# Eight rotations and 152 indexer heads read from matmul banks on VectorE, where a copy in SBUF was read

## The chip, the cores and the metric

One Trainium2 chip, one core. The metric is the device time of one execution in microseconds (us). The kernel before takes 3286.04 us, the median of 3 runs (3277.5 to 3291.01).

The engines are named as the profile names them: PE is the matmul engine (TensorE) and PEld its weight load, DVE is VectorE, ACT is ScalarE, POOL is GpSimd, SP is the engine that issues most of the transfers. PSUM is the memory that matmuls write, in banks of 128 partitions by 512 f32; SBUF is the working memory.

## What is computed

A decoder block over 2048 rows of 1024 channels. What matters here is the indexer of its sparse attention and the rotary embedding ahead of it:

```python
q  = partial_rope(q.reshape(bsz, seq, A_HEADS, HEAD_DIM), cos, sin)
k  = partial_rope(k[:, :, None, :], cos, sin)[:, :, 0]
qi = partial_rope(qi.reshape(bsz, seq, IDX_HEADS, IDX_DIM), cos, sin)
ki = partial_rope(ki[:, :, None, :], cos, sin)[:, :, 0]
...
# partial_rope: rot = [x1 * cos - x2 * sin, x2 * cos + x1 * sin] on 16 of 64 channels
rel   = jax.nn.relu(jnp.einsum('bqhd,bsd->bqhs', qib, ki))      # 4 indexer heads
score = jnp.einsum('bqh,bqhs->bqs', wib, rel)                   # weighted sum over heads
score = jnp.where(causal[None], score, -jnp.inf)
_, sel = lax.top_k(score, topk)                                 # 256 of up to 2048 keys
```

After this come attention over the selected keys, a convolution branch, an output projection, a cross-attention and a gated feed-forward part with a convolution.

## The kernel before, in words

Products are in three terms, of a high and a low part of each operand (`mm3`, lines 275 to 278). A weight tile is loaded, its high part is copied by ACT (L147) and its low part is the difference, on DVE (L152). PSUM has eight banks in four rings: `acc` (3 banks), `tr` (2, transposes), `s` (2) and `o` (1).

**Rotation** (`rotated`, L403 to L416, inside `proj_heads`). For each half of the rows and each of two groups of 512 rows, two pairs of products give the channels to be rotated: the first pair holds the indexer's and the key's channels (rows 0 to 47 of a bank are rotated), the other the queries' (rows 64 to 127). So there are 8 calls. A pair lies in two banks of `acc`, pa and pb. ACT copies both whole banks to SBUF (L406, L407). DVE makes four products with the cosine and sine tables (L410) from these copies, and writes the difference and the sum back over the rotated rows of the copies (L411, L412); what is not rotated is passed on by the copies. Then ACT and DVE split each copy into high and low parts (L147, L152, tile `both`), and SP stores them.

**Indexer scores** (`bg_scores`, L596 to L638). Keys go in stretches of 512; for each block of 128 queries that sees such a stretch there is a piece of four heads. A head is two matmuls into one bank (L615), of `s`, or of `o` for the third head of a piece where `deep` is set; a relu with the absolute weight as scale on ACT, from the bank to an SBUF tile r of a ring of three or four, or two (L617); and on DVE the first head's signed product (L619), or for the others a multiply-add into the sum sc (L621). Then ACT takes the sum apart into 16-bit keys (L633), DVE mends their sign (L634, L635), and SP stores them. `bg_select` loads the keys and searches the threshold by counting, on DVE (L687) or on ACT (L699).

There are 152 heads in three phases. **A**: query blocks 2 to 7, 10 pieces, 40 heads, deep, behind the projections at the start (105 to 215 us of the span). **B**: blocks 8 to 10, 9 pieces, 36 heads, not deep, tiles shared with the selection's (class `Places`, two tiles r), beside the attention of blocks 0 to 7 (up to about 785 us). **C**: blocks 11 to 15, 19 pieces, 76 heads, deep, four tiles r, beside a cross-attention (960 to 1075 us).

**Order of the work.** Each engine takes its queue in order. The program traces generators in turn (`interleave`, `Feed`), by estimated costs; the start, up to about 420 us, is a block whose queues are ordered at build time by a simulated timeline, with a priority for the scores (`later`, offset -SP). From 60 us on POOL works through a depthwise convolution (L958, L959), two instructions for each of 31 taps.

Of the kernel before, what the change touches and what calls it, by code (L numbers as in the profile page):

```python
# [8 lines left out]
F32 = mybir.dt.float32  # L9
# [12 lines left out]
P = 128  # L22
# [39 lines left out]
def hybrid_block(ctx: ExitStack, tc: tile.TileContext, x, mem, positions, norm_mix_g, w_in, w_heads, w_out,  # L62
# [30 lines left out]
    x, mem, out = x[0], mem[0], out[0]  # L93
# [33 lines left out]
    def load_r(dst, src):  # L127
        nc.sync.dma_start(out=dst.bitcast(F32), in_=src.bitcast(F32))
# [7 lines left out]
    def columns(src, h, t0, n):  # L136
        return src[t0 // 1024][:, h, t0 % 1024:t0 % 1024 + n]
# [7 lines left out]
    def split(hi, lo, src, eng=None):  # L145
        with held():
            i = S.activation(out=hi, in_=src, func=AF.Copy)  # L147
            if eng:
                eng.tensor_sub(out=lo, in0=src, in1=hi.bitcast(F32))
                note(S=i)  # L150
            else:
                note(S=i, V=V.tensor_sub(out=lo, in0=src, in1=hi.bitcast(F32)))  # L152
# [134 lines left out]
    def right(name, bufs=2):  # L287
        return tc.tile_pool(name=name, bufs=bufs, side="right", reuse_waits="tile")
# [94 lines left out]
    def proj_heads(ap, hs, half):  # L383
# [4 lines left out]
        RE = (G, V)[1]  # L388
        tabs = {}
# [3 lines left out]
        def send(dst, g, both, pieces):  # L393
            d = dst[half].rearrange("(a p) h t -> (p h) a t", a=2)[:, :, g * 512:(g + 1) * 512]
            for p0, r0, n in pieces:
                store_r(d[r0:r0 + n], both[p0:p0 + n])
# [6 lines left out]
        def rotated(dst, g, pa, pb, rows, pieces_a, pieces_b):  # L403
            ta, tb = (ap.tile([P, 512], F32, name=f"rot{i}", tag="rot", bufs=4) for i in "ab")
            tmps = [ap.tile([P, 512], F32, name=f"rp{i}", tag="rp", bufs=4) for i in range(4)]
            S.activation(out=ta, in_=pa, func=AF.Copy)  # L406
            S.activation(out=tb, in_=pb, func=AF.Copy)  # L407
            x1, x2, cos, sin = ta[rows], tb[rows], tabs[g][rows, 0], tabs[g][rows, 1]
            for o, i0, i1 in zip(tmps, (x1, x2, x2, x1), (cos, sin, cos, sin)):
                RE.tensor_mul(out=o[rows], in0=i0, in1=i1)  # L410
            RE.tensor_sub(out=x1, in0=tmps[0][rows], in1=tmps[1][rows])  # L411
            RE.tensor_add(out=x2, in0=tmps[2][rows], in1=tmps[3][rows])  # L412
            for t, pieces in ((ta, pieces_a), (tb, pieces_b)):
                both = ap.tile([P, 2, 512], F32R, name="both", tag="both", bufs=3)
                split(both[:, 0], both[:, 1], t)
                send(dst, g, both, pieces)  # L416
# [29 lines left out]
        def pair(dst, c0, rows, pieces_a, pieces_b):  # L446
            ws = [load_w(wh_v[:, :, c0 + i * P:c0 + (i + 1) * P]) for i in range(2)]
            for g in range(2):
                pss = []
                for w in ws:  # L450
                    pss.append(acc([P, 512]))
                    yield from product(pss[-1], w, g)
                    if waiting:
                        turn_values(*waiting.pop())
                    if rows is None:
                        plain(dst, g, pss[-1], (pieces_a, pieces_b)[len(pss) - 1])
                if rows is not None:
                    rotated(dst, g, *pss, rows, pieces_a, pieces_b)
# [101 lines left out]


    KP = 0
    SD = (True,4,2,2)

    class Parts:
# [30 lines left out]
    def bg_scores(ip, blks, deep=False, rb=3, sb=2, kb=2):  # L596

        for p0 in range(0, (blks[-1] + 1) * P, 512):
            pw = min(512, (blks[-1] + 1) * P - p0)
            ki2 = [ip.tile([P, 512], F32R, name="ki2", tag=f"ki2{a}", bufs=kb) for a in "ab"]  # L600
            for a in range(2):
                for h in range(2):
                    load_r(ki2[a][h * HD:(h + 1) * HD, :pw], columns(i_d, 4, p0, pw)[a * HD:(a + 1) * HD])
            for b in blks:
                n = (b + 1) * P
                w = min(512, n - p0)
                if w <= 0:
                    continue
                qi = ip.tile([P, NIH, P], F32R, name="qi", tag="qi")
                load_r(qi, columns(i_d, slice(0, NIH), b * P, P))  # L610
                sc = ip.tile([P, 512], F32, name="sc", tag="sc", bufs=sb)
                for h in range(NIH):
                    ps = (acc_o if deep and h % 3 == 2 else acc_s)([P, 512])
                    for a in range(2):
                        PE.matmul(ps[:, :w], qi[:, h, :], ki2[a][:, :w], start=a == 0, stop=a == 1)  # L615
                    r = ip.tile([P, 512], F32, name="r", tag="r", bufs=rb)
                    S.activation(out=r[:, :w], in_=ps[:, :w], func=AF.Relu, scale=absw[:, b, h:h + 1])  # L617
                    if h == 0:
                        V.tensor_scalar(out=sc[:, :w], in0=r[:, :w], scalar1=sgn[:, b, h:h + 1], scalar2=None, op0=ALU.mult)  # L619
                    else:  # L620
                        V.scalar_tensor_tensor(out=sc[:, :w], in0=r[:, :w], scalar=sgn[:, b, h:h + 1], in1=sc[:, :w],  # L621
                                               op0=ALU.mult, op1=ALU.add)
                if n - P >= p0 and n <= p0 + w:
                    V.tensor_add(out=sc[:, w - P:w], in0=sc[:, w - P:w], in1=cb2[:, P:])
                half = sc.bitcast(U16).rearrange("p (s e) -> p s e", e=2)
                hi = ip.tile([P, 512], U16, name="hi_w", tag="hi_w")
                lo = ip.tile([P, 512], U16, name="lo_w", tag="lo_w")
                m7 = ip.tile([P, 512], U16, name="m7", tag="m7", bufs=1)
                for c, a in ((hi, 1), (lo, 0)):
                    if deep and KP > a:  # L630
                        G.tensor_copy(out=c[:, :w], in_=half[:, :w, a])
                    else:
                        S.activation(out=c[:, :w], in_=half[:, :w, a], func=AF.Copy)  # L633
                V.tensor_scalar(out=m7[:, :w], in0=hi[:, :w], scalar1=32768.0, scalar2=32767.0, op0=ALU.is_ge, op1=ALU.mult)  # L634
                V.tensor_tensor(out=hi[:, :w], in0=hi[:, :w], in1=m7[:, :w], op=ALU.bitwise_xor)  # L635
                stq('Y').dma_start(out=key_d[0, b, :, p0:p0 + w], in_=hi[:, :w])
                stq('Y').dma_start(out=key_d[1, b, :, p0:p0 + w], in_=lo[:, :w])
                yield w * 5.5e-3  # L638
# [999 lines left out]
    def w_scores(blks):  # L1638
        return sum((b + 1) * P * 5.5e-3 for b in blks)
# [119 lines left out]
    with tc.block(schedule_with_timeline_sim=True), left("hd") as ap:  # L1759
# [88 lines left out]
        def behind():  # L1848
            with right("ti") as ip:
                yield from later(bg_scores(ip, list(range(2, 8)), True), -SP, False)  # L1850
            ts.append(Scope(right("ts")))
            yield from bg_select(ts[0].pool, *SEL0)
# [11 lines left out]
    with nullcontext() if SB == 8 else right("tx", bufs=1) as tx, right("kv") as kp:  # L1864

        def early_scores():
            drain(sel0)
            yield 0.0
            yield from later(bg_scores(Places(ts[0].pool, tx), list(range(8, SB))), 0, False)

        interleave(bg_attend(list(range(8)), load_kv(kp, 1024, early[1]), lambda b: False, early[2]), w_attend(range(8)), Feed(filler, W_GLU + 50 + 8 + 0 + (44 + -20 if OF0 else 0), 0),
                   Feed(sel0, 3 * w_select(*SEL0)), track.feed(1, 15),
                   *([Feed(early_scores(), 1 * w_scores(range(8, SB)), 40)] if SB > 8 else []))
# [8 lines left out]
    for half in range(2):  # L1882
# [34 lines left out]
        if half == 0:  # L1917
            last = cross(1, xb, hq)
            with right("ti") as ip:
                sc = Feed(bg_scores(ip, list(range(SB, 16)), *SD), 1.65 * w_scores(range(SB, 16)), 0)  # L1920
                done = 0.0
                while sc.live:
                    done += next(last)
                    sc.advance(done, W_CROSS)
# [86 lines left out]
```

## Time and profile before

| what | us |
|---|---|
| median of 3 runs | 3286.04 |
| the profiled execution, its own time | 3288.3 |
| its span in the trace | 3286.5 |
| PE busy | 3073.2 (94%) |
| DVE busy | 2464.3 (75%) |
| ACT busy | 1814.3 (55%) |
| POOL busy | 1339.2 (41%) |

Shares are of the span of one execution. A row of a group of instructions gives line, engine, operation, tiles, shape and count, then the busy time and the mean of one in ns, then the engine's idle time just before them and what ended it.

### The profile page before, as it was taken

Reading aid. Unit: us, or ns where it says so; the run is one execution under the profiler, and the core shown is the slowest. Engines: PE = TensorE matmul, PEld = TensorE weight load, DVE = VectorE, ACT = ScalarE, POOL = GpSimd, SP = SyncE. Lnnn points to the kernel's source line nnn. Section 1 sums busy time; section 2 is a strip of 40 time slices with the busy share of each in tenths; the row PEclk is TensorE's granted clock in tenths of the full one; section 3 lists DMA queues with packets and bytes.
Section 4 is the critical chain, followed back from the end, with each engine's and each line's share of the span. In section 5 each row is a group of like instructions: output and inputs, shape, how many; then the busy total and the mean of one; then the engine's idle time right before and its main releaser. Section 6 shows DMA issues by size and latency. Waiting matters only on the chain.

```text
span 3286.5 us, 45179 instructions
## 1 busy us (share of the span) xinstructions
PE 3073.2 (94%) x16162; PEld 2577.8 (78%) x16162; DVE 2464.3 (75%) x4852; ACT 1814.3 (55%) x3276; POOL 1339.2 (41%) x1141
## 2 busy tenths in 40 slices
PE   7987788998999998999999989999999999999998
PEld 5765577887877787788888878898878777777786
DVE  6899999877758678888788789986555766665445
ACT  7456467655458575667676668775443533333212
POOL 2999703999300799900000038992000144442000
PEclk9988899999999999999999999999999999999999
DMA  7452335543465312121221341103373322222432
GB/s 225 141 157 79 117 106 166 162 152 112 127 196 168 136 46 61 52 61 51 73 70 58 110 156 61 39 20 113 122 256 102 97 88 76 80 77 103 141 103 77
DMA packets 341960, 356.60 MB, mean 109 GB/s; under 512 B 21990, under 2 KB 268518, under 8 KB 340454
## 3 DMA queue, kind: packets, MB, share of 16 engines
q1 hardware_dynamic: 339302, 345.08, 33.2%
q0 software_dynamic: 2432, 8.64, 0.8%
q8 instruction: 127, 2.08, 0.3%
q14 instruction: 99, 0.81, 0.1%
HBM read 271.31 MB, written 82.34 MB: 108 GB/s over the span
## 4 chain that ended last, share of the span: by engine, by line
PE 53%; DVE 29%; ACT 9%; issue 5%; DMA 3%; SPq 0%; POOLq 0%; DVEq 0%; ACTq 0%
PE ps_w L1479 9%; PE ps_acc L276 6%; PE ps_acc L277 6%; PE ps_acc L278 6%; DVE jkc L687 5%; PE ps_s L277 4%; PE ps_s L278 4%; PE ps_s L276 4%; DVE wl L152 3%; ACT junk L699 3%; PE ps_acc L814 3%; DVE xa_cut L1511 2%; PE ps_tr L885 2%; DVE ca L1326 2%; PE ps_o L851 2%
## 5 line engine op out<-in xcount | busy, mean ns | idle before, releaser
L959 POOL TENSOR_TENSOR vt<-pr_c,vt 128x512 f32<-128x512 f32 x480 | 675.3, 1407 | 39.7
L152 DVE TENSOR_TENSOR wl<-raw,wh 128x1024 fp32r<-128x1024 f32 x252 | 335.2, 1331 | 223.1 <-ACT wh L147 217.9
L147 ACT ACTIVATE wh<-raw 128x1024 fp32r<-128x1024 f32 x252 | 264.7, 1051 | 376.5 <-PE ps_acc L278 176.4
L958 POOL TENSOR_SCALAR pr_c<-u,colsB 128x512 f32<-128x512 f32 x480 | 428.1, 892 | 45.1
L276 PE MATMUL ps_acc<-hp,wh 128*128 128x512 f32 x608 | 239.1, 395 | 1.2 <-ACT hp L322 0.8
L277 PE MATMUL ps_acc<-hp,wh 128*128 128x512 f32 x608 | 238.5, 392 | 0.8 <-DVE hp L323 0.8
L278 PE MATMUL ps_acc<-hp,wl 128*128 128x512 f32 x608 | 237.7, 392 | 0.0
L1252 POOL TENSOR_SCALAR xa<-xa,rs_y 128x1024 f32<-128x1024 f32 x4 | 4.4, 1124 | 504.5 <-DVE rs_y L170 504.5
L814 PE MATMUL ps_acc<-kst,qT 128*128 128x512 f32 (+3 forms) x624 | 180.5, 387 | 12.8 <-DVE mx L815 8.9
L836 ACT ACTIVATE prob<-prob,mx 128x1024 f32<-128x1024 f32 (+7 forms) x192 | 172.4, 899 | 27.5 <-DVE mx L815 27.1
L945 POOL DMA_DIRECT2D u<-u_d x16 | 9.3, 583 | 434.9 <-DMA key_d<-hi_w 223.3
L1454 POOL TENSOR_TENSOR hp_cut<-xb_cut 128x512 f32<-128x512 f32 x10 | 17.2, 1718 | 408.6 <-PE ps_tr L1400 352.1
L278 PE MATMUL ps_acc<-hh,wl 128*128 128x512 f32 (+1 forms) x384 | 158.5, 414 | 24.8 <-DVE wl L152 20.7
L317 ACT ACTIVATE pth<-ps_tr 128x512 fp32r<-128x512 f32 (+1 forms) x224 | 126.7, 574 | 91.2 <-PE ps_tr L885 81.7
L276 PE MATMUL ps_acc<-wh,hidh 128*128 128x256 f32 (+1 forms) x512 | 167.6, 327 | 7.1 <-ACT halo L1327 7.1
L1479 PE MATMUL ps_w<-T,wh 128*128 128x512 f32 x496 | 157.3, 399 | 17.9 <-DVE hp_cut L1490 17.9
L318 DVE TENSOR_TENSOR ptl<-ps_tr,pth 128x512 fp32r<-128x512 f32 (+1 forms) x224 | 145.8, 657 | 33.8 <-ACT pth L317 32.2
L276 PE MATMUL ps_acc<-hh,wh 128*128 128x512 f32 (+1 forms) x384 | 156.4, 413 | 15.2 <-ACT wh L147 12.3
L277 PE MATMUL ps_acc<-wl,hidh 128*128 128x256 f32 (+1 forms) x512 | 167.2, 327 | 0.0
L278 PE MATMUL ps_acc<-wh,hidl 128*128 128x256 f32 (+1 forms) x512 | 167.0, 326 | 0.0
L850 PE MATMUL ps_o<-pth,vst 128*128 128x256 f32 x544 | 159.8, 311 | 1.3 <-ACT y_c L991 1.0
L277 PE MATMUL ps_acc<-hl,wh 128*128 128x512 f32 (+1 forms) x384 | 158.8, 414 | 0.0
(479 smaller groups left out, 9891.8 us busy)
## 6 DMA issues: line engine op xcount, KB each, us to landing
raw<-in_w_down_dram SPq DMA_DIRECT2D x44, 512.0 KB
raw<-in_w_up_dram SPq DMA_DIRECT2D x34, 512.0 KB
raw<-in_w_gate_dram SPq DMA_DIRECT2D x34, 512.0 KB
raw<-in_w_out_dram SPq DMA_DIRECT2D x32, 512.0 KB
raw<-in_w_q_cross_dram SPq DMA_DIRECT2D x32, 512.0 KB
raw<-in_w_o_cross_dram SPq DMA_DIRECT2D x32, 512.0 KB
xt<-in_x_dram SPq DMA_DIRECT2D x24, 512.0 KB
raw<-in_w_in_dram SPq DMA_DIRECT2D x24, 512.0 KB
```

The costliest lines, as they stand in the source:

```text
L147: i = S.activation(out=hi, in_=src, func=AF.Copy)
L152: note(S=i, V=V.tensor_sub(out=lo, in0=src, in1=hi.bitcast(F32)))
L276: PE.matmul(ps, ah, bh, start=first, stop=False)
L277: PE.matmul(ps, ah, bl, start=False, stop=False)
L278: return PE.matmul(ps, al, bh, start=False, stop=last).ins
L687: V.tensor_scalar(out=tmp("jkc", n, U16), in0=key, scalar1=cand, scalar2=None, op0=ALU.is_ge, op1=ALU.add, accum_out=cnts[:, r:r + 1])
L814: PE.matmul(ps[:, :w], qT[:, hp * 2 + e, :], ks[p0 // 512][:, a, :w], start=a == 0, stop=a == 1)
L836: S.activation(out=pr, in_=pr, func=AF.Exp, scale=-1.0, bias=st["nm"][:, e:e + 1], accum_out=st["sm"][:, e, pi:pi + 1])
L850: PE.matmul(po, v, pth[:, j - j0, :], start=j == 0, stop=False)
L958: G.tensor_scalar(out=pr, in0=u[:, i:i + 512], scalar1=cb_w(i, c), scalar2=0.0, op0=ALU.mult, op1=ALU.add)
L959: G.tensor_add(out=vt[:, c, :], in0=pr, in1=vt[:, c, :])
L1479: PE.matmul(ps, x[:, k], y[:, k], start=first and k == i == 0, stop=k == 3 and i == 2, skip_group_check=True)
```

## The change

In the rotation, the four products read the rotated rows from the two matmul banks; the copies are still made, and the difference and the sum are written over their rotated rows. In the scores, the relu writes its result over the bank that it reads, and DVE reads the bank; the tile r is no longer allocated.

```diff
             S.activation(out=ta, in_=pa, func=AF.Copy)
             S.activation(out=tb, in_=pb, func=AF.Copy)
-            x1, x2, cos, sin = ta[rows], tb[rows], tabs[g][rows, 0], tabs[g][rows, 1]
+            x1, x2, cos, sin = pa[rows], pb[rows], tabs[g][rows, 0], tabs[g][rows, 1]
             for o, i0, i1 in zip(tmps, (x1, x2, x2, x1), (cos, sin, cos, sin)):
                 RE.tensor_mul(out=o[rows], in0=i0, in1=i1)
-            RE.tensor_sub(out=x1, in0=tmps[0][rows], in1=tmps[1][rows])
-            RE.tensor_add(out=x2, in0=tmps[2][rows], in1=tmps[3][rows])
+            RE.tensor_sub(out=ta[rows], in0=tmps[0][rows], in1=tmps[1][rows])
+            RE.tensor_add(out=tb[rows], in0=tmps[2][rows], in1=tmps[3][rows])
...
+    PR = 1
...
                     ps = (acc_o if deep and h % 3 == 2 else acc_s)([P, 512])
...
-                    r = ip.tile([P, 512], F32, name="r", tag="r", bufs=rb)
+                    r = ps if PR else ip.tile([P, 512], F32, name="r", tag="r", bufs=rb)
                     S.activation(out=r[:, :w], in_=ps[:, :w], func=AF.Relu, scale=absw[:, b, h:h + 1])
```

## Rows read from the trace of the kernel before

**Rows 1.** Busy us of each engine by stretch, then granted clock, DMA share, GB/s

```profile
110.00:160.00 50.00, 48.64 (x215) 39.25 (x213) 46.94 (x47) 25.74 (x43) 46.23 (x37) 1.00 0.46 136
160.00:215.00 55.00, 48.07 (x196) 38.77 (x195) 51.60 (x56) 24.48 (x47) 51.55 (x39) 0.88 0.53 151
215.00:300.00 85.00, 61.29 (x259) 47.32 (x258) 83.00 (x266) 48.98 (x100) 79.04 (x73) 0.86 0.37 105
300.00:420.00 120.00, 97.17 (x407) 73.94 (x406) 117.16 (x246) 71.07 (x154) 87.97 (x68) 0.91 0.38 115
...
740.00:790.00 50.00, 39.07 (x224) 30.33 (x223) 44.05 (x71) 31.77 (x61) 46.46 (x41) 0.97 0.30 90
...
960.00:1075.00 115.00, 111.66 (x543) 90.28 (x542) 93.11 (x189) 90.61 (x176) 0.00 (x0) 1.00 0.52 156
```

**Rows 2.** Waits by who waited for whom, 110 to 420 us: total, times, longest

```profile
PEld ps_acc L278 <- DVE wl L152: 29.6, 12, 6.1
...
PEld ps_tr L379 <- DVE hl L323: 13.7, 4, 10.9
...
PE ps_s L615 <- ACT r L617: 7.5, 4, 2.9
```

**Rows 3.** Groups by line on DVE, 105 to 215 us (phase A)

```profile
L621 DVE SCALAR_TENSOR_TENSOR sc<-r,sgn,sc 128x512 f32<-128x512 f32 (+3 forms) x30 | 34.1, 1137 | 2.0
...
L619 DVE TENSOR_SCALAR sc<-r,sgn 128x512 f32<-128x512 f32 (+3 forms) x10 | 8.8, 879 | 0.7 <-ACT r L617 0.7
```

**Rows 4.** Groups by line and shape on DVE, 960 to 1075 us (phase C)

```profile
L621 DVE SCALAR_TENSOR_TENSOR sc<-r,sgn,sc 128x512 f32<-128x512 f32 x48 | 35.7, 750 | 1.7 <-ACT r L617 0.2
L619 DVE TENSOR_SCALAR sc<-r,sgn 128x512 f32<-128x512 f32 x16 | 7.7, 482 | 0.7 <-ACT r L617 0.7
```

**Rows 5.** Lines 323 and 318, whole span: ns min/median/max, first and last start

```profile
L323 DVE SCALAR_TENSOR_TENSOR hl<-ps_tr,colsA,hh x32: 732/744/753, 17.9 to 311.3; 128x512 fp32r<-128x512 f32 x32
L323 DVE SCALAR_TENSOR_TENSOR ml<-ps_tr,colsA,mh x8: 469/479/484, 575.7 to 582.9; 128x256 fp32r<-128x256 f32 x8
...
L318 DVE TENSOR_TENSOR ptl<-ps_tr,pth x224: 410/684/703, 442.7 to 2538.4; 128x512 fp32r<-128x512 f32 x106, 128x256 fp32r<-128x256 f32 x6
```

**Rows 6.** Groups by line on DVE, 60 to 420 us: the rotation's products

```profile
L410 DVE TENSOR_TENSOR rp<-rotb,tab 48x512 f32<-48x512 f32 (+1 forms) x16 | 18.2, 1177 | 0.1
L410 DVE TENSOR_TENSOR rp<-rota,tab 48x512 f32<-48x512 f32 (+1 forms) x16 | 15.1, 944 | 4.4 <-ACT tab L263 4.3
```

**Rows 7.** Timeline of one head of phase A: start us, us, engine

```profile
152.01 0.62 PE L615 MATMUL ps_o<-ki,qi 128*128 128x512 f32 x2
...
164.40 0.68 ACT L617 ACTIVATE r<-ps_o,absw 128x512 f32<-128x512 f32 x1
...
169.94 2.75 DVE L621 SCALAR_TENSOR_TENSOR sc<-r,sgn,sc 128x512 f32<-128x512 f32 x2
```

**Rows 8.** Timeline of a rotation, 352 to 376 us: first bank copied, last product

```profile
352.44 0.59 ACT L406 ACTIVATE rota<-ps_acc 128x512 f32<-128x512 f32 x1
...
374.61 1.10 DVE L410 TENSOR_TENSOR rp<-rota,tab 64x512 f32<-64x512 f32 x1
```

**Rows 9.** Timeline of one head of phase B

```profile
754.13 0.63 PE L615 MATMUL ps_s<-ki,qi 128*128 128x512 f32 x2
...
756.94 0.85 DVE L619 TENSOR_SCALAR sc<-r,sgn 128x512 f32<-128x512 f32 x1
```

**Rows 10.** Timeline of phase C's first head

```profile
964.85 1.07 PE L615 MATMUL ps_s<-ki,qi 128*128 128x512 f32 x4
...
967.66 0.48 DVE L619 TENSOR_SCALAR sc<-r,sgn 128x512 f32<-128x512 f32 x1
```

**Rows 11.** Groups by line and shape on ACT, whole span: evacuations of a bank

```profile
L317 ACT ACTIVATE pth<-ps_tr 128x512 fp32r<-128x512 f32 x200 | 117.6, 598 | 89.8 <-PE ps_tr L885 80.2 <-PE ps_tr L1183 5.8 <-DVE o L874 1.7
L617 ACT ACTIVATE r<-ps_s,absw 128x512 f32<-128x512 f32 x90 | 59.9, 693 | 13.0 <-PE ps_s L615 6.7 <-DVE rs_y L170 4.1 <-DVE sc L621 1.2
...
L1323 ACT ACTIVATE ca<-ps_acc,colsA 128x512 f32<-128x512 f32 x22 | 16.7, 761 | 0.0
```

## The prediction

> **What bounds the kernel now.** I read the busy time by stretch first, because the change touches three short phases of a long kernel and an average over the span says nothing of them. From 110 to 420 us DVE is busy 298.7 of 310 us (46.94, 51.60, 83.00 and 117.16 added up), 96%, while PE, which is near full elsewhere, falls to 61 of 85 us and 97 of 120 us [rows 1]. There DVE sets the pace. The waits agree: PE's products stand for the low parts of weights (L152) and of the normed input (L323), both made on DVE [rows 2]. In phase C it is the other way round: PE is busy 111.66 of 115 us and DVE 93.11 [rows 1]. Phase B, at 740 to 790 us, is between: DVE 44, PE 39 of 50 us.
>
> Next, what the touched instructions cost in these phases. The multiply-add of a head (L621) takes a mean of 1137 ns in phase A and 750 ns at 512 columns in phase C; the first head's product (L619) 879 and 482 [rows 3, 4]. POOL is busy 46 of 50 and 52 of 55 us in phase A and not at all in phase C [rows 1]. So POOL's convolution, beside it, is what stretches DVE instructions whose tensors both lie in SBUF. Third, the same form with its first tensor in a bank: L323 runs from 18 to 311 us, most of it beside POOL, and takes 732 to 753 ns, with no long one among 32; the plain subtraction L318 takes 684 ns and at most 703 [rows 5]. A bank as first input escapes the stretching. That is the ground of the forecast.
>
> **Part 1, the scores on DVE.** Phase A has 30 multiply-adds and 10 first products. By the code six pieces meet the first 512 keys (one of 384 columns, five of 512) and four the next (128, 256, 384, 512): 6 of 10 are 512 wide, 2 are 384, one 256, one 128. From a bank a multiply-add costs 744 ns at 512 and 479 at 256 [rows 5], so 1.04 ns a column, hence 0.61 us at 384 and 0.35 at 128. Thirty: 18 x 0.744 + 6 x 0.61 + 3 x 0.479 + 3 x 0.35 = 19.5 us, against 34.1 [rows 3]: 14.6 less. The trace shows no first product (L619) that reads a bank. Its bounds are 482 ns, its price now without POOL [rows 4], and 744, the same width with one more tensor [rows 5]. I take 744, since reading 512 columns out of a bank costs 684 even in the plain subtraction: ten cost 6.5 us against 8.8 [rows 3], 2.3 less. Together 16.9 us of DVE time in phase A; with the lower price 19.
>
> In phase C nothing is gained: 750 becomes 744, and 19 first products cost up to 0.26 us more each, 5 us, which lie beside a PE that has the longer work; without that cover they would cost 5. Phase B's gain on DVE, at phase A's rate over 36 heads, would be about 15 us, but it is spread over stretches where PE has other work; I take 2.
>
> **Part 2, the rotation.** The 32 products take 18.2 + 15.1 = 33.3 us [rows 6]. From a bank each costs the plain subtraction's 0.684 [rows 5]: 21.9. Gain 11.4; the first eight, at about 72 to 85 us, lie ahead of the stretch that DVE sets, and a quarter of the count with the least stretching is some 1.5 us of it. So 9.9 count. The difference and the sum still have both inputs in SBUF and stay as they are.
>
> [...] The rows: 744 ns from a bank, 750 from SBUF, the same form and width [rows 4, 5]. [...]
>
> **Part 3, the relu that writes its bank.** No ACT row writes a bank. Bounds: 598 ns, the plain evacuation, and 761, the dearest evacuation to SBUF; now it is 693 [rows 11]. Times 152 heads that is 14 us less or 10 more on ACT, which is busy at most 91 of 115 us in the three phases [rows 1]: hidden. I take no change.
>
> **Part 4, the banks held longer.** This is the price. Now a bank is free once the relu has read it, and the ring of tiles r lets DVE lag; afterwards it is free when DVE has read it. Behind the matmuls of the next head (L615) PE has all its products queued. In phase A the head shown begins on PE at 152.01, ends on ACT at 165.08 and on DVE not before 171 [rows 7]: the hold grows by half. The wait for banks there is 7.5 us on PE already [rows 2]. Lower bound of the addition: none, since the build places matmuls by when their banks come free and DVE is quicker; upper bound: the wait three times over, 15 more, where the hold grows by half. I take 4, half of the present wait. In phase B two banks serve; the hold is 754.13 to 757.79, 3.7 us [rows 9], so a head is possible every 1.85 us. The 36 heads are spread over more than 100 us, and on average that fits; in bursts, a head's matmuls every 0.63 us, each could wait 1.2 us: bounds 0 and 44. I take 3, near the lower end, as part of the hold is a lag that shrinks when PE waits. In phase C the hold is 964.85 to 968.14, 3.3 us [rows 10]. Three of four heads go through two banks, so a bank takes 3 heads of 8 and a head is possible every 3 x 3.3 / 8 = 1.24 us. 76 heads in 115 us need one every 1.5: on average it fits, and the lower bound is none. In bursts, two matmuls every 0.6 us, each head could wait 0.64 us: upper bound 49. I take 4, near the lower end, because cross-attention products stand between the heads and can fill the wait.
>
> For the rotation a bank of three is held until the last product: at 352 to 376 us, 23 us in place of 0.6 [rows 8]. The next pair begins in the third bank, and its second product follows some 6 us later; bounds 0 and 2 us for each of 8. I take none, for DVE and not PE is late there, and it is what would show first if the cover were gone.
>
> **Sum.** In the stretch that DVE sets: 16.9 + 9.9 - 4 = 22.8 us, of which its 96% share, 22, is carried to the end. After it PE has the longer work, so time won stays won. B: 2 - 3 = -1. C: -4. Net 17 us less than the profiled execution's 3288.3, which is 2.3 above the median of the runs: 3288.3 - 17 - 2.3 = **3269 us**, 0.5% less. About 0.5% is also what a measurement of this kernel can tell from no change, so this forecast lies on the line; its own range is 3254 to 3282.
>
> **The rivals.**
>
> *PE waits for banks (slower).* Place: L615 in phase C, where PE is the bound. Price: at the upper bound of phase C 49 us in place of 4, and 8 in place of 3 in B: 50 more than forecast, 3319. It decides from a mean wait of 0.2 us for each of the 112 heads of B and C, which eats the 22 us of phase A. For it: nothing but three banks, and bursts. Against it: matmuls of other parts stand between the heads, and heads already wait behind the relu without much loss. Chance 0.18; half strength gives 3294.
>
> *DVE's gain goes nowhere.* The time is set in phase A by the chain from head to keys to search, not by DVE's sum; DVE idles more. Then only the waits are left of the terms: 3286, or up to 8 more. For it: PE is busy 48.64 of 50 us at 110 to 160 [rows 1], so there both are full. Against it: DVE is 96% busy for 300 us. Chance 0.20.
>
> *The change doesn't do what it says.* The multiply-add has a second tensor and a column in SBUF and stays stretched beside POOL. L323 has both too and isn't stretched. Then 14.6 us fall away: 3283, or 3275 if only half the stretching stays. Chance 0.05.
>
> *More than reckoned.* POOL, disturbed less, ends its taps sooner, fewer other DVE instructions are stretched, and the granted clock of 0.86 to 0.91 [rows 1] comes back as PE idles less: another 15 us, 3254. Chance 0.12.
>
> **How the numbers follow.** The forecast has 0.45. Of it a little over half lies below 3269.6, about 0.26; with the last case and a little of the fourth that is faster 0.40. Slower is most of the first rival, 0.15; the rest, 0.45, is within 0.5%. The range leaves out the bank rival's far end and a tenth on the low side: 3248 to 3302.
>
> **What would show it.** Right: L621 in phase A near 650 ns and never 1700, L410 near 684, DVE's 96% stretch shorter by some 20 us, so that the attention starts earlier; in phase C PE's waits for DVE at L615 of a few us in all. Wrong: L615 waiting for L621 by tens of us, or the stretch from 110 to 420 us as long as before with DVE idle in it.

## The result, and the profile after

| what | before | after |
|---|---|---|
| median of 5 runs, us | 3286.04 | 3267.32 (3263.5 to 3270.41) |
| profiled execution, its own time | 3288.3 | 3263.5 |
| its span | 3286.5 | 3261.7 |
| PE, DVE, ACT, POOL busy | 3073.2, 2464.3, 1814.3, 1339.2 | 3067.2, 2425.8, 1816.6, 1313.1 |

The ratio of the times is 0.9938, with an interval of 0.9927 to 0.9949: 0.6% faster, as forecast and 2 us below the forecast time. From L560 on, a line of the kernel after has a number one higher: the relu is L618, the first product L620, the multiply-add L622, the heads' matmuls L616.

The first check is on single instructions: is an operation that reads a bank free of the stretching beside POOL? These are the groups by line on DVE in the kernel after, from 105 to 215 us, against [rows 3]:

```profile
L622 DVE SCALAR_TENSOR_TENSOR sc<-ps_s,sgn,sc 128x512 f32<-128x512 f32 (+3 forms) x20 | 13.1, 653 | 3.9 <-ACT ps_s L618 3.2
L622 DVE SCALAR_TENSOR_TENSOR sc<-ps_o,sgn,sc 128x512 f32<-128x512 f32 (+3 forms) x10 | 6.6, 657 | 0.4
L620 DVE TENSOR_SCALAR sc<-ps_s,sgn 128x512 f32<-128x512 f32 (+3 forms) x10 | 6.5, 648 | 0.7 <-ACT ps_s L618 0.6
```

and these the instructions of three lines over the whole span (count, then ns min/median/max, first and last start):

```profile
L622 DVE SCALAR_TENSOR_TENSOR sc<-ps_s,sgn,sc x85: 338/742/753, 111.5 to 1057.8; 128x512 f32<-128x512 f32 x62, 128x384 f32<-128x384 f32 x9, 128x128 f32<-128x128 f32 x7, 128x256 f32<-128x256 f32 x7
L620 DVE TENSOR_SCALAR sc<-ps_s,sgn x38: 337/741/752, 110.7 to 1053.7; 128x512 f32<-128x512 f32 x28, 128x384 f32<-128x384 f32 x4, 128x128 f32<-128x128 f32 x3, 128x256 f32<-128x256 f32 x3
L410 DVE TENSOR_TENSOR rp<-ps_acc,tab x32: 670/684/697, 72.5 to 375.6; 48x512 f32<-48x512 f32 x16, 64x512 f32<-64x512 f32 x16
```

The thirty multiply-adds of phase A take 19.7 us in place of 34.1, the ten first products 6.5 in place of 8.8, and the longest of each line is within 2% of its median, though POOL is 46 of 50 us busy beside them. The rotation's products take 684 ns each and keep DVE busy for 20.6 us in all [rows 6: 33.3].

The second check is where the time went. Busy time by stretch in the kernel after (columns as in rows 1):

```profile
110.00:160.00 50.00, 50.00 (x225) 41.16 (x224) 40.15 (x53) 29.93 (x48) 46.21 (x42) 1.00 0.56 162
160.00:215.00 55.00, 54.84 (x257) 45.36 (x256) 47.09 (x76) 27.80 (x51) 51.09 (x44) 1.00 0.63 186
215.00:300.00 85.00, 57.25 (x242) 43.51 (x240) 84.79 (x267) 53.11 (x112) 78.97 (x75) 0.86 0.27 78
300.00:420.00 120.00, 101.36 (x404) 79.09 (x405) 109.95 (x246) 68.06 (x146) 68.77 (x54) 0.89 0.36 108
```

From 110 to 215 us the bound has changed hands. Before, PE was busy 96.7 of 105 us there [rows 1]; now it is busy 104.8, at full clock (1.00 in place of 0.88 in the second half), and DVE has 17.8 us to spare. The attention begins (first exponential) at 428.5 us; in the kernel before it began at 441.0. From 60 us to that point, before and then after:

```profile
60.00:441.00 381.00, 323.55 (x1380) 252.96 (x1380) 344.35 (x716) 200.18 (x395) 308.08 (x252) 0.92 0.43 125
```

```profile
60.00:428.50 368.50, 319.64 (x1384) 252.29 (x1382) 313.52 (x717) 203.15 (x396) 287.26 (x252) 0.93 0.45 130
```

DVE has 30.8 us less to do, the stretch is 12.5 us shorter, and the other 18.3 us have become DVE's idle time (36.7 before, 55.0 after); 11.3 of them lie between 110 and 215 us.

For the later stages I read marks in the two traces: the first exponential of the attention, the first maximum of the cross-attention (end of phase B), and the first multiply-add into the feed-forward part's channels, `ca`, from a bank of `acc` (L1326 before; phase C lies ahead of it).

| stage, us | before | after | difference | forecast |
|---|---|---|---|---|
| start to attention (rotation, phase A) | 441.0 | 428.5 | -12.5 | -22 |
| attention to cross-attention (B) | 363.7 | 357.4 | -6.3 | +1 |
| cross-attention to feed-forward (C) | 339.6 | 338.3 | -1.3 | +4 |
| the rest | 2142.2 | 2137.5 | -4.7 | 0 |

The first three add up to -20.1 where -17 was forecast: the total came out near, and its parts did not. The last row is no finding. Over the single profiles of before, after and the ten kernels below that keep the convolution, the same stretch takes from 2137.5 to 2147.5 us with no order that I can see.

### The profile page after: what moved, and what is told of

Read it like the earlier page. It is cut to its first block, busy times and chain, and to the rows that moved or that the text cites. A ratio compares the mean times of both kernels' runs of the same rounds, so it can differ in the third digit from the quotient of the medians.

```text
span 3261.7 us, 45167 instructions
## 1 busy us (share of the span) xinstructions
PE 3067.2 (94%) x16162; PEld 2578.6 (79%) x16162; DVE 2425.8 (74%) x4852; ACT 1816.6 (56%) x3276; POOL 1313.1 (40%) x1141
## 4 chain that ended last, share of the span: by engine, by line
PE 56%; DVE 27%; ACT 10%; issue 5%; DMA 2%; SPq 0%; POOLq 0%; DVEq 0%; ACTq 0%
PE ps_w L1480 9%; PE ps_acc L276 6%; PE ps_acc L278 6%; PE ps_acc L277 6%; DVE jkc L688 4%; PE ps_s L277 4%; PE ps_s L278 4%; PE ps_s L276 4%; DVE wl L152 3%; ACT junk L700 3%; PE ps_acc L815 3%; DVE xa_cut L1512 2%; PE ps_tr L886 2%; DVE ca L1327 2%; PE ps_o L852 2%
## 5 line engine op out<-in xcount | busy, mean ns | idle before, releaser
L960 POOL TENSOR_TENSOR vt<-pr_c,vt 128x512 f32<-128x512 f32 x480 | 665.3, 1386 | 39.6
L152 DVE TENSOR_TENSOR wl<-raw,wh 128x1024 fp32r<-128x1024 f32 x252 | 339.7, 1349 | 238.2 <-ACT wh L147 235.3
L959 POOL TENSOR_SCALAR pr_c<-u,colsB 128x512 f32<-128x512 f32 x480 | 413.1, 861 | 45.1
L276 PE MATMUL ps_acc<-hh,wh 128*128 128x512 f32 (+1 forms) x384 | 156.9, 414 | 17.1 <-DVE rp L410 10.4
L318 DVE TENSOR_TENSOR ptl<-ps_tr,pth 128x512 fp32r<-128x512 f32 (+1 forms) x224 | 145.6, 655 | 34.7 <-ACT pth L317 33.8
```

What stands on the lines that cost most here:

```text
L276: PE.matmul(ps, ah, bh, start=first, stop=False)
L318: note(S=ins, V=V.tensor_sub(out=lo, in0=ps, in1=hi.bitcast(F32)))
L959: G.tensor_scalar(out=pr, in0=u[:, i:i + 512], scalar1=cb_w(i, c), scalar2=0.0, op0=ALU.mult, op1=ALU.add)
L960: G.tensor_add(out=vt[:, c, :], in0=pr, in1=vt[:, c, :])
```

## The experiments

The theory: what is gained is relief of DVE from POOL, and what is paid is banks held longer. The rivals: that one part carries the whole gain and the other nothing, and that the gain has another source than POOL (another order of the queues, for one). Each kernel was timed in five rounds against the kernel before, which took 3289.58 us in the first batch (rotation alone, scores alone, A alone, rotation with A and B), 3289.77 in the second (B alone, the two without the convolution, the one without copies) and 3293.6 in the third, on another chip (the others). Across batches I compare ratios.

### The rotation alone, the scores alone

The first keeps the rotation's part of the change and gives the relu its tile r back:

```diff
-    PR = 1
+    PR = 0
```

> Only the rotation reads the banks; the scores keep their tile r. Stretching theory: the 32 products fall from 33.3 to about 22 us, of which some 9 reach the end: 3277, and L619/L621 stay stretched in phase A (near 1100 ns). Reordering theory (the gain comes from another order of the queues, not from shorter instructions): no relation to the 11 us, between 3265 and 3290. Banks theory (acc banks held too long): 3286 or more, with PE waiting for L410.

The second keeps the scores' part and lets the rotation read its copies again:

```diff
-            x1, x2, cos, sin = pa[rows], pb[rows], tabs[g][rows, 0], tabs[g][rows, 1]
+            x1, x2, cos, sin = ta[rows], tb[rows], tabs[g][rows, 0], tabs[g][rows, 1]
```

> All 152 heads use the bank, the rotation reads its copies as before. Less a_only this gives B and C together. Stretching theory: B has POOL beside it and gains some us, C has none and loses at most a few: 3270 to 3276. Banks theory: B and C lose, so this is slower than a_only by 5 us or more.

The rotation alone: 3295.55 us, ratio 1.0012 [1.0003, 1.0022], 0.1% slower. The scores alone: 3271.88 us, 0.994 [0.9927, 0.9954], as good as the whole change within the intervals.

The rotation alone gained nothing where 3277 us was expected; the heads stay stretched, 1212 ns for a multiply-add of phase A. DVE did get faster at its products: L410 takes 20.6 us there too. But PE waits for it. PE's and PEld's waits for it from 60 to 435 us (in us, how often, the longest), first in the kernel with the rotation alone:

```profile
PE ps_acc L276 <- DVE rp L410: 19.2, 5, 8.5
PEld ps_acc L276 <- DVE rp L410: 10.7, 2, 8.8
```

and in the kernel after:

```profile
PE ps_acc L276 <- DVE rp L410: 10.4, 2, 6.3
```

PEld's waits are the same pauses, seen at the weight load (from 200 to 300 us it is one of 8.8 us on PEld and one of 8.5 on PE), so the two are not added up: PE waits 19.2 us and 10.4 us.

One such wait in the rotation-only kernel, from its timelines of ACT, DVE and PE (start, us, engine; in brackets the idle time and what ended it):

```profile
359.18 0.60 ACT L406 ACTIVATE rota<-ps_acc 128x512 f32<-128x512 f32 x1 [3.49 <-PE ps_acc L278]
371.12 0.57 ACT L407 ACTIVATE rotb<-ps_acc 128x512 f32<-128x512 f32 x1
...
361.06 0.69 DVE L410 TENSOR_TENSOR rp<-ps_acc,tab 64x512 f32<-64x512 f32 x1
374.10 1.91 DVE L410 TENSOR_TENSOR rp<-ps_acc,tab 64x512 f32<-64x512 f32 x3
...
369.95 0.39 PE L278 MATMUL ps_acc<-hh,wl 128*128 128x512 f32 x1
375.54 0.77 PE L276 MATMUL ps_acc<-hh,wh 128*128 128x512 f32 x1 [5.20 <-DVE rp L410]
376.11 0.63 PE L277 MATMUL ps_acc<-hl,wh 128*128 128x512 f32 x1
```

The first bank is copied by 359.8 us, the second by 371.7; before the change each would, by the program, have been free then. Here PE's next product wants a bank at 370.3 and gets it at 375.5, when DVE has come round to its products, 13 us after the first of them. The matmuls that follow the pause take 0.63 us in place of 0.39. This is the row of the `acc` banks that the forecast priced at nothing.

### Phase A alone, B alone, both, and the rotation with both

```diff
-                    r = ps if PR else ip.tile([P, 512], F32, name="r", tag="r", bufs=rb)
+                    r = ps if blks[0] in (2,) else ip.tile([P, 512], F32, name="r", tag="r", bufs=rb)
```

The tuple is (2,) for phase A, (8,) for B, (2, 8) for both; a phase is known by its first query block. The first three also have the rotation reading its copies; the fourth has (2, 8) and the change's rotation.

> Only the 40 heads of phase A (blocks 2 to 7) use the bank; rotation, B and C as before. Stretching theory: L619 and L621 in phase A fall from 42.9 to about 26 us, the attention starts 10 to 14 us earlier, 3273. Banks theory: PE waits for DVE at L615 take back half or more: 3280 or above. Reordering theory: no relation.

> Only the 36 heads of phase B (blocks 8 to 10, beside the attention of blocks 0 to 7) use the bank; rotation, A and C as before. scores_only less a_only left 13 us to B and C, where B was reckoned at 1. Theory that B carries them: 3274 to 3280, and the stage from the first exponential to the first maximum of the cross-attention is 5 to 8 us shorter than the 364 us of the kernel before. Theory that parts do not add up and B is worth 1: 3286 to 3292.

> Only the heads of phases A and B use the bank; the rotation reads its copies, C keeps its tile r. Alone, A gave 6 and B 5 us; with the rotation, which alone costs 4, they gave 23. Theory that A and B help each other (less stretching in both, and one common order of queues): 3266 to 3272 where before is 3290. Theory that the parts simply add: 3276 to 3281, and the rotation is then worth 10 us in company.

> Rotation, A and B use the banks, C keeps its tile r. Against the changed kernel (3267) this is the price of C alone. Stretching theory: C has no POOL beside it, so nothing is gained there and its first products get dearer: this is 0 to 6 us faster than the changed kernel, 3261 to 3267. Theory that C gains too (relu to a bank quicker, less work in order): this is 2 to 6 us slower, 3269 to 3273.

| kernel | us | ratio, interval | to attention | B's stage | C's stage |
|---|---|---|---|---|---|
| before | | | 441.0 | 363.7 | 339.6 |
| rotation alone | 3295.55 | 1.0012 [1.0003, 1.0022] | 442.1 | 367.7 | 339.2 |
| A alone | 3284.77 | 0.9982 [0.9973, 0.9992] | 434.1 | 367.1 | 339.1 |
| B alone | 3284.56 | 0.9984 [0.9976, 0.9993] | 442.5 | 359.1 | 341.0 |
| A, B | 3279.93 | 0.9963 [0.9948, 0.9977] | 437.1 | 359.3 | 341.3 |
| rotation, A, B | 3268.91 | 0.993 [0.9916, 0.9944] | 430.2 | 359.0 | 340.0 |
| A, B, C (scores alone) | 3271.88 | 0.994 [0.9927, 0.9954] | 434.2 | 359.0 | 338.0 |
| the change | 3267.32 | 0.9938 [0.9927, 0.9949] | 428.5 | 357.4 | 338.3 |

The stages are from one profile of each kernel, the ratios from several runs. A alone fell short of its expectation: 3284.77 us where 3273 was expected, with the attention 7 us earlier in place of 10 to 14. A and B alone and together simply add up (6, 5 and 12 us). B's stage takes 357 to 359 us in the five kernels of the table that have B and 364 to 368 in the three that have not: B seems worth 4 us or more there, and B alone gains 5 us in the ratio (0.16% of 3290). It is not a clean rule: the three without B spread by 4 us themselves, and the kernel with two banks below, whose phase B is that of the change, takes 363.8. The source of B's gain is the same as A's: groups by line on DVE in the kernel with B alone, 428 to 805 us,

```profile
L622 DVE SCALAR_TENSOR_TENSOR sc<-ps_s,sgn,sc 128x512 f32<-128x512 f32 (+3 forms) x27 | 17.7, 654 | 1.7 <-ACT ps_s L618 1.7
L620 DVE TENSOR_SCALAR sc<-ps_s,sgn 128x512 f32<-128x512 f32 (+3 forms) x9 | 5.9, 656 | 0.8 <-ACT ps_s L618 0.8
```

and the same groups of the kernel before:

```profile
L621 DVE SCALAR_TENSOR_TENSOR sc<-r,sgn,sc 128x512 f32<-128x512 f32 (+3 forms) x27 | 25.5, 948 | 0.6 <-ACT r L617 0.4
L619 DVE TENSOR_SCALAR sc<-r,sgn 128x512 f32<-128x512 f32 (+3 forms) x9 | 5.9, 651 | 0.7 <-ACT r L617 0.7
```

7.8 us less on DVE, not the 15 that phase A's rate would give, and of those the stage keeps 4.6. The wait for banks that I set against it is there, but small. All waits of PE and PEld for the products, 428 to 790 us, in the kernel after:

```profile
PEld ps_s L616 <- DVE sc L622: 7.7, 8, 2.7
PE ps_s L616 <- DVE sc L622: 4.8, 5, 2.0
PEld ps_s L616 <- DVE sc L620: 2.7, 3, 2.1
PE ps_s L616 <- DVE sc L620: 1.9, 1, 1.9
```

PE's part is 6.7 us for 36 heads, and it replaces 2.9 us of waiting for the relu: 3.8 more, where I took 3.

To the attention the rotation brings nothing by itself (442.1 against 441.0), and 6 to 7 us on top of A (437.1 without it and 430.2 with it where A and B use the banks, 434.2 and 428.5 where A, B and C do). Part of it may be that DVE, with less to do for the heads, comes to the rotation's products sooner: PE waits 19.2 us for L410 with the rotation alone and 10.4 in the change. But another wait moves in the same kernels. PE's transposes for the rotation's tables (L262) read a tile, `rep`, part of which a fill of 0.1 us on POOL writes (L255), and that fill stands in POOL's queue behind the taps. PE's waits for it from 60 to 435 us, first with A alone, then in the change:

```profile
PE ps_tr L262 <- POOL rep L255: 16.6, 1, 16.6
```

```profile
PE ps_tr L262 <- POOL rep L255: 8.4, 1, 8.4
```

It is 16.6 us with A and B and 11.0 with the scores alone, 4.1 with the rotation on top of A and B, and 0.2 at most in the kernel before, with B alone and with the rotation alone. With A alone the chain of work that ended last goes through POOL's taps to this fill:

```profile
273.60 1.26 POOL vt L960
274.86 0.10 POOL rep L255
275.00 1.97 PE ps_tr L262 x8
```

and so it does with A and B, with the scores alone and with two banks (below), and in no other kernel here. So where the heads of A are relieved and the rotation is not, PE comes to these transposes before POOL has come to the fill, and this, beside the banks, can be why A alone fell short. No run separates the two. It also meets a rival: POOL's own work is quicker in the change, so its convolution could have carried the gain by ending sooner. In the kernels before and after, that chain has no instruction of POOL between 60 and 1140 us.

The ratios, too, show a gain of the rotation on top of A and B, 0.9963 against 0.993, but not on top of A, B and C, 0.994 against 0.9938. By the medians C's part is worth some 7 us where the rotation is not there (0.9963 against 0.994; the intervals overlap) and nothing where it is (0.993 against 0.9938). This stays open: C's own stage shows 2 to 3 us, and each variant has its queues ordered anew at build time. How much such an order can move shows here too: the kernel with A and B and the one with all three phases differ in C alone, and yet their attention begins 2.9 us apart.

### The convolution taken away

If the gain is relief from POOL, it must vanish where POOL is idle. Both kernels, before and after, without 29 of the 30 further taps of each channel group (so that the convolution's output is another; the first of the 31 taps is one instruction on POOL, the others are two):

```diff
-                if onpool:
+                if onpool and i > 1:
+                    pass
+                elif onpool:
```

> The kernel before with 29 of the 30 further taps of each convolution channel group left out on POOL, so that POOL is nearly idle; the convolution's output is another. Stretching theory: L619, L621 and L410 take in all phases what they take in phase C (482, 750, 684 ns), and the time falls by 20 us or more. Reordering theory: durations fall too, but the time need not.

> The changed kernel with the same taps left out. Stretching theory: with POOL idle the change has nothing to give, so this is within 5 us of before_notaps, or slower by the wait for banks. Reordering theory: it is faster than before_notaps by about as much as with the taps, 15 to 20 us.

Without the taps the kernel before takes 3161.36 us, 0.9612 [0.9598, 0.9625], and the kernel after 3170.73, 0.9638 [0.9625, 0.9651]. The intervals touch only at their ends: the change now costs about 9 us, 0.3%. So nothing of the gain is left without POOL's taps, and the price that goes with it is visible when there is nothing to relieve. Beside POOL the change gains 20 us (0.62% of 3290); if the price is the same there, which no run shows, the relief is worth some 29. The instructions without the taps (groups on DVE, 60 to 395 us, of the kernel before without taps):

```profile
L621 DVE SCALAR_TENSOR_TENSOR sc<-r,sgn,sc 128x512 f32<-128x512 f32 (+3 forms) x30 | 21.3, 712 | 12.2 <-ACT r L617 10.7
L410 DVE TENSOR_TENSOR rp<-rota,tab 48x512 f32<-48x512 f32 (+1 forms) x16 | 10.9, 684 | 5.2 <-ACT tab L263 5.1
L410 DVE TENSOR_TENSOR rp<-rotb,tab 48x512 f32<-48x512 f32 (+1 forms) x16 | 10.3, 682 | 1.5 <-ACT rotb L407 1.4
L619 DVE TENSOR_SCALAR sc<-r,sgn 128x512 f32<-128x512 f32 (+3 forms) x10 | 6.3, 627 | 2.4 <-ACT r L617 2.3
```

The multiply-add in SBUF takes 712 ns in place of 1137. Over these four groups the change saves DVE 29.4 us with the taps (76.2 to 46.8) and 2.0 without them (48.8 to 46.8). The attention begins at 378.3 us without the change and at 389.3 with it: the price lies in the first stretch, 11 us. I had expected to find it as waits; mostly it is not there. PE waits 6.0 us for L410, and for the banks of the heads no wait shows. Most of it seems to be in the order of PE's queue. The heads' matmuls into `ps_s` in phase A (count, ns, first and last start), the kernel before without taps,

```profile
L615 PE MATMUL ps_s<-ki,qi x60: 222/392/397, 105.9 to 188.2; 128*128 128x512 f32 x36, 128*128 128x384 f32 x12, 128*128 128x128 f32 x6, 128*128 128x256 f32 x6
```

the kernel after without taps,

```profile
L616 PE MATMUL ps_s<-ki,qi x60: 220/393/397, 101.9 to 200.3; 128*128 128x512 f32 x36, 128*128 128x384 f32 x12, 128*128 128x128 f32 x6, 128*128 128x256 f32 x6
```

the kernel after with its taps,

```profile
L616 PE MATMUL ps_s<-ki,qi x60: 220/393/397, 101.8 to 200.6; 128*128 128x512 f32 x36, 128*128 128x384 f32 x12, 128*128 128x128 f32 x6, 128*128 128x256 f32 x6
```

and the kernel before with its taps:

```profile
L615 PE MATMUL ps_s<-ki,qi x60: 273/393/580, 106.4 to 204.4; 128*128 128x512 f32 x36, 128*128 128x384 f32 x12, 128*128 128x128 f32 x6, 128*128 128x256 f32 x6
```

With the change the last head's matmul starts at 200.3 or 200.6 us, whether POOL works or not; without it and without the taps, at 188.2. PE is full in these three (104 or 105 of 105 us from 110 to 215). I read this from the program, and no run shows it by itself: the build's timeline holds a bank until DVE has read it, and so sets the heads further apart, with other products between them. Without the taps the search for the threshold then begins at 211.1 in place of 198.8 us. With the taps the kernel before has its last head at 204.4: there the relief outweighs the price, and the search begins at 210.5 with the change in place of 217.7.

### Fewer banks, and the banks used evenly

If the order follows the banks, their number must show. All heads through the two banks of `s`:

```diff
-                    ps = (acc_o if deep and h % 3 == 2 else acc_s)([P, 512])
+                    ps = acc_s([P, 512])
```

> The changed kernel with all heads in the two banks of ring s, none in o, so that a bank comes round after 2 heads in place of 8/3. Theory that the hold of the banks is a price of about 10 us paid mostly in phase A, where the search begins no earlier with POOL idle: the search begins 3 to 8 us later than 210 and C loses a few us, in all 5 to 15 us slower than the changed kernel, 3273 to 3285. Theory that the banks of the scores cost nothing: no change, 3266 to 3271.

3277.6 us, 0.9961 [0.9947, 0.9975]: by the ratios 7 to 8 us slower than the change (the intervals just touch). Its heads in phase A:

```profile
L616 PE MATMUL ps_s<-ki,qi x80: 222/393/397, 102.1 to 229.0; 128*128 128x512 f32 x48, 128*128 128x384 f32 x16, 128*128 128x128 f32 x8, 128*128 128x256 f32 x8
```

The last starts at 229.0, the search at 242.4 in place of 210.5, far later than the 3 to 8 us expected, with PE full (105.00 of 105 us). In the change, three heads of four go through `s`: a bank of `s` takes 15 heads from 101.8 to 200.6 us, one each 6.6 us; here 20 heads from 102.1 to 229.0, one each 6.3. By this a bank's turn seems to set the pace of the heads. The lost time itself is not shown to be the banks' alone: PE's wait for POOL's fill (`rep`) is 17.0 us here, against 8.4 in the change. Two further kernels aim at the banks. One orders the rotation's products so that x1, and with it the first bank, is done after two of them; the other does so and sends every third head through `o`, counted across pieces:

```diff
-            for o, i0, i1 in zip(tmps, (x1, x2, x2, x1), (cos, sin, cos, sin)):
+            for o, i0, i1 in zip((tmps[0], tmps[3], tmps[1], tmps[2]), (x1, x1, x2, x2), (cos, sin, sin, cos)):
```

```diff
+    ring3 = [-1]
...
-                    ps = (acc_o if deep and h % 3 == 2 else acc_s)([P, 512])
+                    ring3[0] += 1
+                    ps = (acc_o if deep and ring3[0] % 3 == 2 else acc_s)([P, 512])
```

> The changed kernel with the four products of a rotation in another order: both from the first bank, then both from the second, so that the first bank is read before the second's product need be done. PE waits there for L410 10.4 us of its queue's time (19.2 with the rotation alone changed). Theory that this hold eats the rotation's gain: the wait falls by half and the time by 2 to 6 us against the changed kernel, 3262 to 3267. Theory that DVE's backlog sets when any product runs: the wait and the time stay.

> early_free, and the heads of A and C dealt evenly over the three banks by one counter (two to s, one to o) in place of three to s and one to o. Theory that the hold of the score banks costs: the search begins 1 to 4 us earlier and another 2 to 5 us are gained on early_free. Theory that PE's own work sets phase A now: same as early_free within 3 us.

The order of the products: 3265.94 us, 0.9923 [0.9908, 0.9937]. With the even use of banks: 3262.61 us, 0.9914 [0.99, 0.9929]. In the first PE's wait for L410 falls from 10.4 to 4.1 us, by more than half, as the theory of the hold expected, and its time by the ratios by some 5 us; but the intervals overlap, so by time it can't be told from the change. Its heads, and then those of the second:

```profile
L616 PE MATMUL ps_s<-ki,qi x60: 226/393/477, 105.5 to 198.6; 128*128 128x512 f32 x36, 128*128 128x384 f32 x12, 128*128 128x128 f32 x6, 128*128 128x256 f32 x6
```

```profile
L618 PE MATMUL ps_s<-ki,qi x54: 275/393/397, 105.2 to 196.0; 128*128 128x512 f32 x32, 128*128 128x384 f32 x10, 128*128 128x128 f32 x6, 128*128 128x256 f32 x6
L618 PE MATMUL ps_o<-ki,qi x26: 278/393/411, 105.9 to 190.9; 128*128 128x512 f32 x16, 128*128 128x384 f32 x6, 128*128 128x128 f32 x2, 128*128 128x256 f32 x2
```

The second differs from the first in the use of the banks alone, so the first is what it must be compared with. The heads take 90.8 us in place of 93.1, the search begins at 206.6 us in place of 210.9, the attention at 424.0 in place of 426.9. The heads' 2.3 us are less than kernels with the same turns differ among themselves (93.1 us here, 99.0 with the rotation, A and B), PE's wait for POOL's fill fell as well, from 8.2 to 0.3 us, and the intervals of the times overlap. So fewer banks set the heads apart by far more than a new order does, but it is not shown that the even use of the three gives anything back. This kernel is the fastest of all that were run with the convolution; against the change its interval still touches (0.9929 and 0.9927), in another batch.

### Without the copies

If reading the bank is good, the two copies of the rotation might go altogether. The difference and the sum are written into the banks, which are then split into high and low parts as any product is:

```diff
-            ta, tb = (ap.tile([P, 512], F32, name=f"rot{i}", tag="rot", bufs=4) for i in "ab")
...
-            S.activation(out=ta, in_=pa, func=AF.Copy)
-            S.activation(out=tb, in_=pb, func=AF.Copy)
...
-            RE.tensor_sub(out=ta[rows], in0=tmps[0][rows], in1=tmps[1][rows])
-            RE.tensor_add(out=tb[rows], in0=tmps[2][rows], in1=tmps[3][rows])
...
+            RE.tensor_sub(out=x1, in0=tmps[0][rows], in1=tmps[1][rows])
+            RE.tensor_add(out=x2, in0=tmps[2][rows], in1=tmps[3][rows])
+            for ps, pieces in ((pa, pieces_a), (pb, pieces_b)):
+                plain(dst, g, ps, pieces)
```

> The changed kernel, with the rotated channels written back into the two matmul banks and split from there; the two copies by ACT (L406, L407) are gone. 16 copies of 0.59 us on ACT go and 16 splits on DVE fall from some 1.0 to 0.68 us. Theory that DVE and ACT set the pace of the start: 3 to 8 us faster than the changed kernel, 3260 to 3266 where before is 3288. Theory that PE is the bound in the start now, or that the banks of the products are held too long: the same or slower.

3276.68 us, 0.996 [0.9948, 0.9973]: faster than before, by the ratios slower than the change by about 7 us (the intervals just touch). DVE has less to do from 60 to 420 us (289.3 us, against 306.4 in the kernel after), and yet the attention begins at 437.1. PE's waits from 60 to 435 us in this kernel (L318 makes the low part from the bank):

```profile
PE ps_acc L278 <- DVE wl L152: 24.9, 7, 12.1
PE ps_acc L276 <- DVE both L318: 13.1, 3, 8.2
```

The banks are held longer still, and PE waits 13.1 us for their last reader, in place of 10.4. Its wait for the weights' low parts (L152) is longer too, 24.9 us against 14.0 in the change, and why is not shown. The trade is the same: less work on DVE, a later attention.

## Why the prediction was right, and where its steps were not

The time fell by about what was forecast and lies inside the range. The mechanism was the one named; that the total came so near was luck, as its parts were off in both directions.

**The mechanism held.** The step "a bank as first input escapes the stretching", taken from L323, is what the runs show: 742 ns and never over 753 beside POOL, and the gain gone once POOL is idle. In phase A the multiply-add takes 1137 ns on average with both tensors in SBUF [rows 3], 653 and 657 with one in a bank, 712 with both in SBUF but without the taps.

**The instruction prices held.** Thirty multiply-adds: 19.5 forecast, 19.7 measured; ten first products: 6.5 and 6.5; 32 rotation products: 21.9 and 20.6. For the multiply-add a bank came out no dearer than SBUF: L622 takes 742 to 743 ns by the medians (84 of its 114 are 512 wide), and at 512 columns in phase C 745 and 746 on average, against 750 at 512 from SBUF [rows 4]. Reading the bank made the first product dearer where POOL is idle, as bounded: 745 against 482 ns in phase C, 4 us of DVE time behind a full PE.

**The relu** came out a little on the cheap side of its bounds: 660 ns at the median, 687 before, on an ACT that isn't the bound.

```profile
L618 ACT ACTIVATE ps_s<-ps_s,absw x123: 323/660/713, 110.2 to 1055.7; 128x512 f32<-128x512 f32 x90, 128x384 f32<-128x384 f32 x13, 128x128 f32<-128x128 f32 x10, 128x256 f32<-128x256 f32 x10
```

**The step that failed first** is "the stretch that DVE sets ... its 96% share, 22, is carried to the end". 12.5 us arrived. I had read DVE as the bound for the whole 310 us, though [rows 1] show PE at 48.64 of 50 us already in the first 50. With 11 us less on DVE from 110 to 215 us, PE was full there, and what else DVE saved became idle time. Further on PE stops for 8.4 us at POOL's fill (`rep`), a wait of 0.2 us before, and for 10.4 us at L410; what each of these costs to the end is not shown. The rival "DVE's gain goes nowhere" named that row; it was half right.

**The second** is the price of the banks, "I take 4" in phase A and "I take none" for the rotation. Together they cost about 11 us at the start of the attention with the taps away, where the two are not separated. And the form was wrong: I looked for waits at L615, and in phase A of the change PE has 0.2 us of them; without the taps there is none, and the heads stand further apart in PE's queue instead. For the rotation the cover that I named (DVE and not PE is late there) was not there: PE waits 10.4 us in the change and 19.2 with the rotation alone, whose attention begins no earlier than before.

**The third** is phase B, "2 - 3". The wait was sized rightly (3.8), but the gain of 2 was taken by judgement where the rows gave a DVE time; 7.8 us of DVE time were saved, and the stage became 4 to 6 us shorter. In C the 4 us set down for waits did not come: PE's and PEld's waits at L616 for DVE's reading of a score, from 940 to 1075 us, are 0.8 and 4.9 us, and PE is busy 113.42 of the 115 us from 960 on, where it was 111.66 [rows 1].

**The errors cancelled**: 9.5 us too much in the first stage, 7 too little in B, 5 too little in C. The 28.8 us of relief and the 11 of price that were summed up look close to 29 and 9, but the 29 is the measured gain and the price without taps added up, and not measured by itself. The mechanism was understood, stage by stage the sum was not, and that it came out is luck.

## What to carry to other kernels

Where a VectorE instruction with two SBUF inputs runs beside a busy GpSimd, leave one input in its matmul bank: here that took a quarter to two fifths off each such instruction (the rotation's products from 944 and 1177 ns on average to 684, the multiply-add of phase A from 1137 to 653 and 657). Then ask who holds the bank now and how many banks share the turns, for a price can be paid in the order of the queues, where no view of waits shows it; compare the first and last start of the matmuls that use those banks. Do not add a matmul's wait to its weight load's: here they were the same pauses. Look, too, for short instructions queued behind a long job on an engine off the path: a fill of 0.1 us on POOL stopped PE for up to 17 us. And before carrying a saving on one engine to the end, look at how full the next engine is in the same stretch, not only over the phase.

## What was not expected of the hardware

- The relu that writes over its own bank is quicker than the one that writes SBUF: at 512 columns 663 against 693 ns on average [rows 11].
- POOL is relieved as well: its 480 products and 480 sums of the convolution take 861 and 1386 ns on average, where they took 892 and 1407, 25 us less over the kernel.
- The first product, with a single SBUF tensor, is stretched beside POOL too: 879 ns on average over four widths in phase A, 627 over the same without the taps; 512 columns take 482 in phase C, without POOL [rows 3, 4]. From a bank it takes 752 at most.
- The granted clock from 160 to 215 us rose from 0.88 to 1.00, with PE busy 54.84 us of 55 in place of 48.07 [rows 1].
